# Two stages of a two-layer trunk in another order: the first key product beside the gates, and RWKV's weight halves cast one segment earlier

## Chip, core and metric

The kernel runs on one core of one Trainium2 chip, as one launch. The metric is the device time of that launch in microseconds (us); lower is better. Before the change it is 2180.25 us, the median of three runs (2178.22 to 2181.9).

The engines are named as the profile names them: PE is the matrix engine (PEld its weight loads), DVE the vector engine, ACT the scalar engine, POOL the fourth compute engine, and SP the engine whose queue issues nearly all DMAs here. Each engine works through its own instructions in program order; it waits, with everything queued behind, whenever the next instruction needs something that another engine or a DMA has not yet delivered.

## What is computed

One inference step of a two-layer trunk, for one prompt of 16 + 1024 tokens and for 8 decoding sequences of 8 tokens (1104 token columns in all, cut into three segments of 384, 384 and 336). Layer 0 is gated DeltaNet, layer 1 is RWKV-7. Cut to what matters here:

```python
def gdn_mixer(xn, S0, conv_buf, w_in, ...):          # layer 0
    proj = xn @ w_in
    qkv, z, b, a = ...                               # q, k, v, output gate, two gates per head
    qkv, new_buf = causal_conv(qkv, conv_buf, conv_w)   # 4 taps, then silu
    q, k = l2norm(q), l2norm(k)
    beta = jax.nn.sigmoid(b)
    g = -jnp.exp(a_log) * jax.nn.softplus(a + dt_bias)
    gc = jnp.cumsum(g)                               # within a chunk
    decay = jnp.exp(gc[i] - gc[j])
    A = I + strict(beta * k @ k.T * decay)
    u, wk = triangular_solve(A, ...)                 # per chunk and head
    ...                                              # state recurrence over the chunks
def rwkv_mixer(xn, ...):                             # layer 1
    xs = xn + (xprev - xn) * mu                      # six token-shift mixes
    r, k, v, z = (xs[m] @ w_rkvz[m] for m in range(4))
    ...                                              # decay, delta recurrence, group norm, gate, w_o
```

## The kernel before

All activations are kept with the tokens along the free axis. A product with a weight matrix is written as three passes that together give nearly full float32 precision: the weight is split into a rounded part `whi` and a rest `wlo`, the input likewise (`xa`, `xc` and others hold the parts), and one 128-wide block of output channels over one segment is 24 matmuls (8 blocks of the contraction, three passes each). A weight half (4 blocks, tile `wraw`, 256 KB) is loaded by SP, cast to `whi` by ACT (line 87) and subtracted to `wlo` by POOL (line 91).

**The start of layer 0** (`layer0`). The input rows are normed and transposed, then `gates` (lines 350 to 406) makes the per-head decays. Its first step multiplies all three segments by the 48 gate columns (tile `d`, copied to `rows`); its second transposes `rows` (PE tile `fgt`) and computes `g` on DVE and ACT (`gx`, `gy`, `gb`, `gs`); its third takes the cumulative sums on PE (`fgc`, `mge`) and copies them to `gc` on DVE (line 388); its fourth transposes `gc` (PE tile `fgr`), copies that to `gr` on DVE (lines 401 and 402) and writes it to DRAM (`drow`, SP lines 405 and 406). From `drow` SP loads, broadcast over rows, the tile `E` (line 649); POOL masks it (affine selects, lines 653 to 658), ACT takes the exponentials, and DVE multiplies it by the key scores `fsc` (line 712). The result goes through DRAM (`ltd`, line 718) into the tile `invA`, of which `inverse32` (lines 573 and 575) makes 32-wide triangular inverses in 31 steps of two DVE instructions each. DVE copies the result (line 743), SP sends it through DRAM (`g_t`, `T1n`, lines 746 and 749), and PE merges the blocks (tile `rY`), after which PE's products go on.

Beside that, the first head pair's products run: `keys` (PE tile `dk`), `gdn_queries` (`dq`), `gdn_values` (`dv`). Each segment's result is copied by ACT to `raw`, convolved (one tap on ACT, three on DVE, tile `cvy`, line 526), and squashed to `K`, `Q` or `vt` (line 532). The order is set by hand: PE and ACT run under a manual schedule, `self.slot` counts half segments of products, and `gdn_events` fastens the other steps (the gate steps, the scores, the inverse) to slot numbers. The first product starts at slot -24. `history` and `history_turn` load and turn the old convolution rows (`hist`, `histT`). The convolution tiles live in the pool `fp`, which is opened by `gdn_front` after the input rows (`x0` to `x8`) have been given up.

**The projections of layer 1** (`layer1`, `projections`). 24 blocks (m, k) of the weights for r, v and z run on PE, tile `d`, each for two or three segments. The weights come by halves: `weights(n + 1, 0)` is called at a block's first segment and `weights(n + 1, 1)` at its last, each a load by SP, a cast by ACT and a subtraction by POOL; `whi` and `wlo` have three buffers each, which all halves share. The results are copied to `ev` by ACT (line 2354) and stored. Into this stream a planner's numbers (`LOWER`, `END`) put the making of the RWKV inverses (tiles `sldcak`, `ssq`, `fL`). The recurrence itself, the wave, follows (`wave`), and opens with transfers that SP issues in program order: folds (`fld2c`, `fldrv`), `AR`, `BK`, `rTT`, and the old states `sn`.

## Time and profile before

| | |
|---|---|
| runs of the kernel | 2180.25 us median (2178.22 to 2181.9, three runs) |
| profiled execution | 2173.21 us, of which the span is 2171.5 us |
| mean granted PE clock | 0.982 |
| busy: PE, DVE, ACT, POOL | 2046.2, 1583.4, 1283.1, 834.9 us |
| instructions in the span | 54811 |
| DMA traffic | 292.52 MB, 135 GB/s on average |

The span is what the trace covers; the profiled execution is 1.7 us longer. A row of a timeline reads: start, busy time, engine and line, operation, output and inputs, tile shapes, count of like instructions merged, and in brackets the engine's idle time just before and what ended it. A row of windows reads: the stretch, its length, then busy time and instruction count of PE, PEld, DVE, ACT and POOL, the granted PE clock, the share of time that the DMA engines were busy, and GB/s.

### The profile page before, as it was taken

The page shows a single profiled execution, that of the slowest core. Times are in us where ns is not written, and L with a number is a line of the kernel's source. Part 1 is how long each engine was busy: PE and PEld are TensorE (multiplying, and loading weights), DVE is VectorE, ACT ScalarE, POOL GpSimd, SP SyncE. Part 2 cuts the span into 40 slices and gives each one's busy share as a digit, 9 for nine tenths or more (in the row PEclk, how much of TensorE's full clock was granted, in tenths as well). Part 3 has the DMA queues.
Part 4 walks back from the last instruction along what each step waited for, and adds up shares of the span by engine and source line. Part 5 has one row for each costly group of instructions (what it writes and reads, how often), then busy time and mean ns, then how long its engine had stood idle before and what let it go on. Part 6 is the DMA issues. An engine that isn't in the chain of part 4 may idle for free. (4 is left out here: it accounts for less than half of the span.)

```text
span 2171.5 us, 54811 instructions
## 1 busy us (share of the span) xinstructions
PE 2046.2 (94%) x20418; PEld 1905.8 (88%) x20418; DVE 1583.4 (73%) x4212; ACT 1283.1 (59%) x3750; POOL 834.9 (38%) x1136
## 2 busy tenths in 40 slices
PE   6969899999999999999999999889899999999997
PEld 5959899999999999998899999889798988888876
DVE  6968879698888979795334676757979557767755
ACT  4536565656565665656533365664747446677774
POOL 3523334334343333334231352344524254444444
PEclk9979999999999999999999999999999999999999
DMA  3424343424333333335345115655555486677754
GB/s 120 122 58 105 77 108 90 118 79 107 90 97 106 106 97 104 97 102 159 106 129 135 63 54 191 220 160 174 169 180 158 117 224 175 188 234 225 228 178 139
DMA packets 430724, 292.52 MB, mean 135 GB/s; under 512 B 147337, under 2 KB 413050, under 8 KB 430458
## 3 DMA queue, kind: packets, MB, share of 16 engines
q1 hardware_dynamic: 430458, 289.02, 46.2%
q8 instruction: 161, 2.64, 0.5%
q14 instruction: 105, 0.86, 0.1%
HBM read 197.55 MB, written 91.37 MB: 133 GB/s over the span
## 5 line engine op out<-in xcount | busy, mean ns | idle before, releaser
L91 POOL TENSOR_TENSOR wlo<-wraw,whi 128x512 fp32r<-128x512 f32 (+1 forms) x246 | 331.1, 1348 | 465.6 <-ACT whi L87 413.9
L77 PE MATMUL d<-xc,whi 128*128 128x384 f32 (+2 forms) x1006 | 279.5, 337 | 4.8 <-ACT whi L87 4.1
L526 DVE SCALAR_TENSOR_TENSOR cvy<-raw,cw,cvy 128x408 f32<-128x408 f32 (+2 forms) x288 | 199.0, 692 | 17.1 <-ACT cvy L63 15.7
L87 ACT CAST whi<-wraw 128x512 fp32r<-128x512 f32 (+1 forms) x246 | 149.8, 611 | 88.1 <-PE d L77 51.2
L77 PEld LDWEIGHTS d<-xc,whi 128*128 128x128 f32 (+1 forms) x1006 | 183.4, 189 | 7.8 <-ACT whi L87 4.8
L77 PE MATMUL d<-xc,wlo 128*128 128x384 f32 (+3 forms) x476 | 157.7, 340 | 2.7 <-POOL wlo L91 2.7
L77 PE MATMUL dz<-xc,whi 128*128 128x384 f32 (+1 forms) x480 | 153.9, 338 | 0.0
L77 PE MATMUL dv<-xc,whi 128*128 128x384 f32 (+1 forms) x480 | 152.4, 337 | 0.0
L77 PE MATMUL d<-xa,whi 128*128 128x384 f32 (+3 forms) x450 | 142.1, 340 | 4.5 <-ACT whi L87 1.7
L63 ACT ACTIVATE o<-rA,gcol 128x128 f32<-128x128 f32 x128 | 42.0, 366 | 116.9 <-DVE S L905 116.7
L573 DVE TENSOR_TENSOR invtmp<-invA,invT 72x31 f32<-72x31 f32 (+15 forms) x248 | 102.2, 412 | 3.2
L77 PE MATMUL dv<-xa,whi 128*128 128x384 f32 (+1 forms) x288 | 99.1, 344 | 0.0
L77 PE MATMUL dz<-xa,whi 128*128 128x384 f32 (+1 forms) x288 | 98.6, 342 | 0.0
L575 DVE TENSOR_TENSOR invT<-invT,invtmp 72x31 f32<-72x31 f32 (+15 forms) x248 | 95.0, 383 | 3.3
L77 PEld LDWEIGHTS d<-xc,wlo 128*128 128x128 f32 (+1 forms) x476 | 89.3, 189 | 6.8 <-POOL wlo L91 3.6
L77 PEld LDWEIGHTS dz<-xc,whi 128*128 128x128 f32 x480 | 89.4, 189 | 4.6 <-issue 4.5
L77 PEld LDWEIGHTS d<-xa,whi 128*128 128x128 f32 (+1 forms) x450 | 83.9, 189 | 8.2 <-issue 3.7
L77 PEld LDWEIGHTS dv<-xc,whi 128*128 128x128 f32 x480 | 89.2, 188 | 1.4 <-issue 1.4
L77 PE MATMUL d<-xa,wlo 128*128 128x384 f32 (+3 forms) x252 | 84.9, 337 | 1.4 <-POOL wlo L91 1.4
L77 PE MATMUL dk<-xc,whi 128*128 128x384 f32 (+1 forms) x240 | 79.3, 349 | 0.0
L77 PE MATMUL dq<-xc,whi 128*128 128x384 f32 (+1 forms) x240 | 77.0, 338 | 0.0
L1335 DVE SCALAR_TENSOR_TENSOR mixs<-xb,pcol,mixs 128x320 f32<-128x320 f32 (+2 forms) x96 | 68.6, 725 | 5.9 <-ACT mixs L63 5.6
(542 smaller groups left out, 6801.0 us busy)
## 6 DMA issues: line engine op xcount, KB each, us to landing
wraw<-in_gdn_w_in SPq DMA_DIRECT2D x96, 256.0 KB
wraw<-in_rwkv_w_rkvz SPq DMA_DIRECT2D x80, 256.0 KB
Sb<-in_state_gdn SPq DMA_DIRECT2D x64, 256.0 KB
sldcak<-cakd SPq DMA_DIRECT2D x24, 576.0 KB
wraw<-in_rwkv_w_o SPq DMA_DIRECT2D x42, 256.0 KB
E<-drow SPq DMA_DIRECT2D x24, 384.0 KB
attn<-drow SPq DMA_DIRECT2D x24, 384.0 KB
wraw<-in_gdn_w_out SPq DMA_DIRECT2D x36, 256.0 KB
```

The costliest lines, as they stand in the source:

```text
L63: return self.nc.scalar.activation(out, in_, func, bias=bias, scale=scale, **kw)
L77: self.nc.tensor.matmul(out, lhsT, rhs, start=start, stop=stop)
L87: nc.scalar.copy(hi, x)
L91: e.tensor_tensor(lo, x, hi.bitcast(F32), op=ALU.subtract)
L526: nc.vector.scalar_tensor_tensor(y[0][:, 0:wd], raw[:, k:k + wd], cw[k], y[0][:, 0:wd], op0=ALU.mult, op1=ALU.add)
L573: nc.vector.tensor_tensor(tmp, A[:, j, j + 1:32].unsqueeze(2).broadcast_to([nb, n, m]), Tv[:, j, 0:m].unsqueeze(1).broadcast_to([nb, n, m] ...
L575: nc.vector.tensor_tensor(Tv[:, j + 1:32, 0:m], Tv[:, j + 1:32, 0:m], tmp, op=ALU.subtract)
L1335: nc.vector.scalar_tensor_tensor(x[:, f:], xb[:, 8 + a + f:8 + b], mu, x[:, f:], op0=ALU.mult, op1=ALU.add)
```

## The change

Two independent parts. Line numbers after the change are 1 to 27 higher than before.

**Part A, start of layer 0.** `gates` now yields after each of its three segments. `layer0` runs the gates' first segment, then both halves of the first key product's first segment, then the gates' other two segments, then the three remaining gate steps, then the rest of the key product; `products` skips this product, so the slots start at -18 and all later slot numbers stay. For this the first key weights are loaded ahead of the input norm, and the convolution tiles get a pool of their own (`gconv`, opened first), so that they need not wait for the input rows' room; `x0` to `x8` are allocated ahead.

**Part B, projections of layer 1.** The load (`fetch`) is separated from the cast and the subtraction (`weights`), which run at high priority. Every second block's second half has its own pair of buffers, so there are four in all; `weights(n + 1, 1)` runs at segment 1 (of 0 to 2, or of 0 and 1 for z), and the next block's first half is already loaded then.

```diff
@@ gates
     for s, (c0, n) in enumerate(SEGS):
         p = self.dense(w, 64, xh, xl, s)
         nc.scalar.copy(rows[:, c0:c0 + n], p[0:48, 0:n])
-    yield
+        yield
@@ history, history_turn, last_tokens, conv (hist, histT, last, raw, cvy alike)
-        r = t(self.fp, [108, 128], "hist", 1)[0:96]
+        r = t(self.cvp, [108, 128], "hist", 1)[0:96]
@@ build
+            self.cvx = ExitStack()
+            self.cvp = self.cvx.enter_context(tc.tile_pool(name="gconv", bufs=1, side="right", reuse_waits="tile"))
@@ layer0
         self.gates_open(gates)
+        self.raw_weights(1024)
         self.input_norm(hi, lo)
         self.inp.close()
         self.gdn_front(front)
-        self.raw_weights(1024)
...
-        gate = self.gates(kh, kl)
-        next(gate)
...
         self.history_turn(G[0].H)
+        gate, first = self.gates(kh, kl), G[0].keys(0)
+        for n in range(3):
+            next(gate)
+            if not n:
+                next(first)
+                next(first)
+        for _ in range(3):
+            next(gate, None)
+        for _ in first:
+            pass
...
             for n, (_, f) in enumerate(todo):
-                yield from f(todo[n + 1][0] if n + 1 < len(todo) else None)
+                if n:
+                    yield from f(todo[n + 1][0] if n + 1 < len(todo) else None)
...
-        before(-24)
+        before(-18)
...
-            self.slot = -24
+            self.slot = -18
@@ layer1
-        def weights(n, h, elo="first"):
+        raw = {}
+
+        def fetch(n, h):
             if n < 25:
                 m, k = (todo + [(3, 0)])[n]
-                (hi,), (lo,) = self.load_w(..., 4, elo=elo)
-                W[n, h] = hi, lo
+                raw[n, h] = self.load_w(..., 4, later=True)[0]
+
+        def weights(n, h):
+            if n < 25:
+                if (n, h) not in raw:
+                    fetch(n, h)
+                own = n % 2 and h
+                hi, lo = W[n, h] = [t(self.own if own else self.wp, [128, 4, 128], a, 1 if own else 3, F32R) for a in ("whi", "wlo")]
+                with tc.high_priority():
+                    self.split(raw.pop((n, h)), hi, lo)
...
-        ip = pool("rinv", ctx)
+        ip = self.own = pool("rinv", ctx)
...
                     if s == 0:
                         weights(n + 1, 0)
-                    if s == segs[m] - 1:
+                        fetch(n + 1, 1)
+                    if s == 1:
                         weights(n + 1, 1)
+                        if n < 23:
+                            fetch(n + 2, 0)
```

How the instructions stand now, at three places. A row gives line, operation, output and inputs with buffer numbers, and size; `x2` and the like merge equal neighbours. In all, the order differs by few instructions: the work is the same but for one or two weight halves' position.

**Place 1, start of layer 0.** On PE, before, the cumulative sums stand in the middle of the key product's second segment (`dk_589`), between its two halves:

```order
L77 MATMUL dk_589<-xc_107,whi_375 128x384
L77 MATMUL fgc_606<-g_556,upto_27_152 128x16
L77 MATMUL fgc_606<-g_556,upto_28_153 128x128
L77 MATMUL fgc_606<-g_556,past_29_154 128x16
L77 MATMUL fgc_606<-g_556,past_30_155 128x128
L77 MATMUL mge_613<-gs_564,ones_82 128x144
L77 MATMUL mge_613<-g_556,ones_82 128x128
L77 MATMUL dk_589<-xc_107,whi_379 128x384
L77 MATMUL dk_589<-xc_107,wlo_380 128x384
```

Now they stand in the first query product (`dq_728`), behind the whole key product:

```order
L77 MATMUL dq_728<-xa_112,wlo_621 128x384
L77 MATMUL dq_728<-xc_116,whi_620 128x384
L77 MATMUL dq_728<-xc_116,whi_660 128x384
L77 MATMUL fgc_584<-g_573,upto_27_155 128x16
L77 MATMUL fgc_584<-g_573,upto_28_156 128x128
L77 MATMUL fgc_584<-g_573,past_29_157 128x16
L77 MATMUL fgc_584<-g_573,past_30_158 128x128
L77 MATMUL mge_591<-gs_581,ones_91 128x144
L77 MATMUL mge_591<-g_573,ones_91 128x128
L77 MATMUL dq_728<-xc_116,wlo_661 128x384
```

So 12 matmuls of `dk`'s second segment, the 24 of its third and 13 of `dq`'s first segment have come ahead of `fgc` (and 32 `dk` matmuls ahead of the last `fgt`). The two `fgr` rows, before between `dk`'s second and third segment, now stand in the middle of `dq`'s second segment. On DVE, before, `gc` and `gr` follow directly on the first key segment's convolution (`cvy_582`):

```order
L526 SCALAR_TENSOR_TENSOR cvy_582<-raw_521,cw_404,cvy_582 128x408 x3
L388 COPY gc_611<-fgc_606 128x9x8x2
L401 COPY gr_641<-fgr_638 128x128
L402 COPY gr_641<-fgr_638 16x128
L526 SCALAR_TENSOR_TENSOR cvy_633<-raw_587,cw_404,cvy_633 128x384
L532 SCALAR_TENSOR_TENSOR K_648<-raw_521,cvy_582 128x64
L532 SCALAR_TENSOR_TENSOR K_648<-raw_521,cvy_582 128x320
L526 SCALAR_TENSOR_TENSOR cvy_633<-raw_587,cw_404,cvy_633 128x384
L507 COPY raw_718<-histT_508 128x8x3
```

Now they stand behind the convolutions of all three key segments (`cvy_637` and `cvy_677` are the second and third) and the first tap of the query's (`cvy_756`):

```order
L533 SCALAR_TENSOR_TENSOR K_645<-raw_502,cvy_637 128x384
L527 SCALAR_TENSOR_TENSOR cvy_677<-raw_642,cw_407,cvy_677 128x336 x3
L389 COPY gc_589<-fgc_584 128x9x8x2
L533 SCALAR_TENSOR_TENSOR K_684<-raw_642,cvy_677 128x336
L527 SCALAR_TENSOR_TENSOR cvy_756<-raw_725,cw_407,cvy_756 128x408
L402 COPY gr_601<-fgr_598 128x128
L403 COPY gr_601<-fgr_598 16x128
L527 SCALAR_TENSOR_TENSOR cvy_756<-raw_725,cw_407,cvy_756 128x408
L703 SCALAR_TENSOR_TENSOR fsc_786,kq_692<-fsc_786,ident_83 128x128
```

DVE's set of instructions from there to the inverse's end (line 743) is the same as before; the scores of the second segment (line 702) now come ahead of the first multiplication of `E`.

**Place 2, start of layer 1's projections, ACT.** Before, the copy of the first result (`ev_18355`) stands ahead of a table load and the norms of the first inverse (`sldcak`, `ssq`):

```order
L87 CAST xh_2705_15356<-mixs_19021 128x384
L87 CAST xh_2707_15358<-mixs_19071 128x384
L2354 COPY ev_18355<-d_18296 128x384
L63 ACTIVATE mixs_19175<-xb_2604_14337,omu_411 128x64
L63 ACTIVATE mixs_19175<-xb_2604_14337,omu_411 128x320
L63 ACT_TABLE_LOAD
L63 ACTIVATE sldcak_18319<-sldcak_18319 128x383
L63 ACTIVATE ssq_18325<-sldcak_18319 128x384
L63 ACTIVATE mixs_19231<-xb_2602_14335,omu_411 128x384
```

Now a weight cast (`whi_18382`) comes first, and the copy (`ev_18361`) stands behind the table load:

```order
L87 CAST whi_18382<-wraw_18359 128x512
L87 CAST xa_112<-mixs_18278 128x336
L63 ACTIVATE mixs_19083<-xb_2603_14340,omu_414 128x64
L63 ACTIVATE mixs_19083<-xb_2603_14340,omu_414 128x320
L87 CAST xh_2705_15360<-mixs_19027 128x384
L87 CAST xh_2707_15362<-mixs_19083 128x384
L63 ACT_TABLE_LOAD
L63 ACTIVATE sldcak_18323<-sldcak_18323 128x383
L63 ACTIVATE ssq_18329<-sldcak_18323 128x384
L63 ACTIVATE mixs_19181<-xb_2604_14341,omu_414 128x64
L63 ACTIVATE mixs_19181<-xb_2604_14341,omu_414 128x320
L2381 COPY ev_18361<-d_18300 128x384
```

From here on each cast on ACT, each `wlo` on POOL and each load on SP of the projections stands at the same place as before but holds the next half.

**Place 3, opening of layer 1's wave, SP.** Before, one load of a weight half (`wraw_23107`) stands among the loads of the states `sn`, and two follow them (`ev_23101` is a result of the last projection):

```order
L1959 DMA sn_23182<-in_state_rwkv 64x4x64
L205 DMA wraw_23107<-in_rwkv_w_rkvz 128x4x128
L1959 DMA sn_23182<-in_state_rwkv 64x4x64
L2355 DMA zd<-ev_23101 128x384
L1959 DMA sn_23182<-in_state_rwkv 64x4x64 x2
L205 DMA wraw_23198<-in_rwkv_w_rkvz 128x4x128
L205 DMA wraw_23204<-in_rwkv_w_rkvz 128x4x128
L1555 DMA fldrv_23265<-rvd 128x2x384
L1709 DMA AR_23267<-abd 128x384
L1710 DMA BK_23268<-abd 128x6x64
```

Now the four `sn` come first, and two weight halves stand ahead of the first `rTT` and the folds:

```order
L1960 DMA sn_23186<-in_state_rwkv 64x4x64 x4
L2382 DMA zd<-ev_23105 128x384
L205 DMA wraw_23202<-in_rwkv_w_rkvz 128x4x128
L205 DMA wraw_23208<-in_rwkv_w_rkvz 128x4x128
L1730 DMA rTT_3859_23171<-ttd 128x384
L1556 DMA fld2c_23267<-cakd 128x2x384
L1556 DMA fldrv_23269<-rvd 128x2x384
L1710 DMA AR_23271<-abd 128x384
L1711 DMA BK_23272<-abd 128x6x64
```

On POOL, the `wlo` that stood ahead of the copies to `DC` (which need `fld2c`) is gone from there, so that the next `wlo` stands behind them.

More of the change, by code (lines that the diff above doesn't have):

```diff
@@ L270, in input_open @@
         self.xrows = []
+        self.xt = [self.t(self.lp, [128, D], f"x{q}") for q in range(9)]
     def input_load(self, qs):
         for q in qs:
-            x = self.t(self.lp, [128, D], f"x{q}")
+            x = self.xt[q]
             self.xrows.append((x, self.rows_of_x(x, q)))
@@ L481, in history_turn @@
         self.transpose(p[:, 0:96], H.raw)
-        H.old = self.t(self.fp, [128, 4, 8, 3], "histT", 1)
+        H.old = self.t(self.cvp, [128, 4, 8, 3], "histT", 1)
         self.nc.vector.tensor_copy(H.old.rearrange("p u b r -> p (u b r)"), p[:, 0:96])
@@ L488, in last_tokens @@
         self.transpose(p[0:108, 0:128], H.last.rearrange("p u b -> p (u b)"))
-        ls = self.t(self.fp, [108, 128], "hist", 1)
+        ls = self.t(self.cvp, [108, 128], "hist", 1)
         nc.vector.tensor_copy(ls, p[0:108, 0:128])
@@ L503, in begin @@
             if u == 0:
-                H.last = t(self.fp, [128, 4, 27], "last", 1)
-            raws[0] = raw = t(self.fp, [128, 411], "raw", 3)
+                H.last = t(self.cvp, [128, 4, 27], "last", 1)
+            raws[0] = raw = t(self.cvp, [128, 411], "raw", 3)
             sv = raw[:, 0:88].rearrange("p (b r) -> p b r", r=11)
@@ L512, in follow @@
             if s < 2:
-                raws[s + 1] = t(self.fp, [128, 411], "raw", 3)
+                raws[s + 1] = t(self.cvp, [128, 411], "raw", 3)
                 nc.gpsimd.tensor_copy(raws[s + 1][:, 0:3], prev)
@@ L522, in taps @@
                 nc.gpsimd.tensor_copy(H.last[:, u, 0:24].rearrange("p (b r) -> p b r", r=3), sv[:, :, 8:11])
-            y.append(t(self.fp, [128, 408], "cvy", 2))
+            y.append(t(self.cvp, [128, 408], "cvy", 2))
             self.act(y[0][:, 0:wd], raw[:, 0:wd], AF.Identity, scale=cw[0])
@@ L2205, in layer0 @@
         front.close()
+        self.cvx.close()
         before(999)
@@ L2253, in layer1 @@
         self.rwkv_masks(self.ev, None)
+        t = self.t
         todo = [(m, k) for m in (0, 2, 3) for k in range(8)]
@@ L2263, in part @@
             self.mix_part(m, k, c0, c0 + n, xb[k], *self.slots[order[m][k]], self.ev, lows[m])
-        def weights(n, h, elo="first"):
+        raw = {}
+        def fetch(n, h):
             if n < 25:
                 m, k = (todo + [(3, 0)])[n]
-                (hi,), (lo,) = self.load_w(self.i["rwkv_w_rkvz"][0, m][512 * h:512 * h + 512, 128 * k:128 * k + 128], 4, elo=elo)
-                W[n, h] = hi, lo
+                raw[n, h] = self.load_w(self.i["rwkv_w_rkvz"][0, m][512 * h:512 * h + 512, 128 * k:128 * k + 128], 4, later=True)[0]
+        def weights(n, h):
[6 more added lines that the diff above has]
+                    self.split(raw.pop((n, h)), hi, lo)
         def between(k):
@@ L2365, in layer1 @@
         b_now = [-1]
-        t = self.t
         with tc.manual_schedule(engines={mybir.EngineType.PE}):
```

## The prediction

> **What bounds the kernel now.** The page's first table says PE: 2046.2 of 2171.5 us. That is an average; what counts is where PE is not busy, and whether the change touches that. I read the windows first (length, then busy time and count of PE, PEld, DVE, ACT, POOL, then PE clock, DMA share, GB/s).
>
> ```profile
> 0.00:41.00 41.00, 22.20 (x130) 18.57 (x131) 28.80 (x60) 22.82 (x43) 14.99 (x47) 0.96 0.52 157
> 41.00:60.00 19.00, 18.56 (x122) 17.47 (x121) 7.71 (x20) 9.07 (x20) 2.50 (x6) 1.00 0.10 28
> 60.00:128.19 68.19, 50.60 (x357) 47.60 (x355) 66.09 (x177) 29.22 (x81) 32.22 (x46) 0.92 0.36 96
> 60.00:70.00 10.00, 9.93 (x62) 9.61 (x61) 9.75 (x19) 5.55 (x16) 6.98 (x14) 1.00 0.96 290
> 113.00:133.00 20.00, 0.38 (x4) 0.14 (x2) 15.16 (x39) 1.10 (x6) 3.43 (x3) 0.61 0.19 49
> 1745.00:1780.00 35.00, 31.62 (x303) 27.24 (x303) 21.19 (x48) 15.76 (x37) 17.18 (x23) 0.95 0.99 271
> ```
>
> Part A lies in the rows up to 133, the opening of RWKV's wave, which part B's loads touch, in the last. From 113 to 133 PE stands still, and the timelines of PE and DVE say for what:
>
> ```profile
> 133.43 0.31 PE L77 MATMUL rY<-T1n,E 32*32 32x32 f32 x2 [20.05 <-DMA T1n<-g_t]
> 70.77 1.65 DVE L712 SCALAR_TENSOR_TENSOR E<-fsc,bp,E 128x128 f32<-128x128 f32 x6
> 89.70 0.17 DVE L573 TENSOR_TENSOR invtmp<-invA,invT 72x31 f32<-72x31 f32 x1
> 128.19 1.03 DVE L743 COPY invA<-invT 72x1024 f32<-72x1024 f32 x1
> ```
>
> PE waits 20.05 us for the inverse, which ends on DVE at 128.19, and 5.2 us of copy and DMA later PE goes on. So until 133 **DVE is the bound**, not PE. DVE is busy 66.09 of 68.19 us after 60, and its timeline shows no wait there; between 41 and 60 it is busy 7.71 of 19, idle 11.3. Moving key matmuls ahead gains only if it moves the inverse's end; PE's own time in this stage is covered by the 20 us.
>
> **Part A, step by step.** The key product's 36 matmuls and 13 of the query product come ahead of the cumulative sums `fgc`.
>
> ```profile
> 47.23 0.38 PE L74 MATMUL fgt<-ident,rows 48*128 48x48 f32 x3 [0.44 <-ACT rows L362]
> 51.88 0.60 PE L77 MATMUL fgc<-g,upto 128*128 128x16 f32 x4
> 55.45 0.40 PE L77 MATMUL dk<-xa,whi 128*128 128x336 f32 x1
> 59.21 0.33 PE L77 MATMUL dq<-xa,whi 128*128 128x384 f32 x1
> 60.96 0.33 PE L77 MATMUL dq<-xa,wlo 128*128 128x384 f32 x1
> 39.47 0.37 PE L77 MATMUL d<-xa,whi 128*64 128x336 f32 x1 [0.72 <-ACT xa L305]
> 33.12 0.39 PE L77 MATMUL d<-xc,whi 128*64 128x384 f32 x1 [0.61 <-DVE xc L309]
> ```
>
> The third segment's 24 matmuls take 59.21 - 55.45 = 3.8 us. The row at 60.96 is the eleventh of `dq`, ten intervals after 59.21: 0.175 each. So `fgc` moves by 25 x 0.175 + 3.8 = 8.2 us, less the PE idle that the earlier `dk` matmuls fill, at most 0.61 + 0.72 + 0.44 = 1.8: `fgc` at about 58.3 instead of 51.88. The cumulative sum is then copied on DVE, in before at once, now behind three taps of the third key segment, which wait for ACT:
>
> ```profile
> 54.62 0.30 DVE L388 COPY gc<-fgc 128x144 f32<-128x144 f32 x1
> 63.62 3.58 DVE L526 SCALAR_TENSOR_TENSOR cvy<-raw,cw,cvy 128x336 f32<-128x336 f32 x3
> 55.24 1.28 ACT L63 ACT_TABLE_LOAD   x1
> 56.54 0.66 ACT L63 ACTIVATE eglb<-mge 128x272 f32<-128x272 f32 x1
> 57.97 0.62 ACT L63 ACTIVATE cvy<-raw,cw 128x384 f32<-128x384 f32 x1
> 58.49 0.53 ACT L63 ACTIVATE raw<-cvy 128x408 f32<-128x408 f32 x1
> 56.06 0.36 SPq L405 DMA_DIRECT2D drow<-gr  x1
> 62.14 1.14 POOL L653 TENSOR_SCALAR_AFFINE_SELECT E<-E 128x768 f32<-128x768 f32 x1 [0.48 <-DMA E<-drow]
> 64.53 0.85 POOL L653 TENSOR_SCALAR_AFFINE_SELECT E<-E 128x768 f32<-128x768 f32 x1
> 68.16 1.86 ACT L63 ACTIVATE E<-E,gcol 128x128 f32<-128x128 f32 x6
> 69.33 0.30 DVE L702 SCALAR_TENSOR_TENSOR fsc<-fsc,ident 128x128 f32<-128x128 f32 x1
> ```
>
> In the new order ACT has, after the third tap of the second segment (about 58.2, just ahead of `gs`), a table load 1.28, a tanh 0.53 and a first tap 0.6: 60.6. Three taps at 0.6 (as for the other forms; 3.58 for three is a disturbed row, below) end at 62.4: `gc` there, 8 us later than in before. `fgr` is in PE's order 20 `dq` matmuls behind `mge`, at about 63.3, so it isn't late. Then `gr` stands on DVE behind `K` and the query's first tap, which needs ACT's next steps (a tanh 0.53, `eglb` and three short ones about 1.0, the query's copies about 0.5, a tap 0.6): 65.0; the tap 0.6 and the copies 0.5 on DVE follow, and `drow` is sent at about **66.0 instead of 56.06**.
>
> From there the trace has one path: `drow` out, `E` in, POOL's select at 62.14 (6.1 us after `drow`), 1.14 for it, an exponential of 0.31 (1.86 for six): the first multiplication of `E` can start 7.6 us after `drow`. In before that was 63.7, and DVE came to it at 70.77, 7 us of slack. Now it is 73.6 at the soonest. At 60 to 70 the DMAs are loaded, so I take 0.7 more, **74.3, or +3.5 us**; the ends are +0.3 (`gc` not held by the taps, `drow` at 63.5) and +5.5.
>
> Behind that DVE has the same work left as in before's 57.4 us (70.77 to 128.19), less what is already done, plus new waits. Done already: the second segment's scores, three at 0.3, each with a read of 0.1, and three small steps, -1.6. New waits: two sets of `E` now follow each other, and a set needs 0.85 on POOL and six exponentials on ACT against 1.65 on DVE, +1.0; the first step of the inverse (89.70) comes to wait for `invA`, issued at 86.04 in before, +1.1; two taps that DVE reaches early, +0.8. The waits are estimates from the order of these rows; together 0 to 4. The front's sum: 3.5 - 1.6 + 2.9 = **+4.8 us**, with ends -1 and +8. PE's stall gets shorter by what PE arrives later, and PE goes on 4.8 us later. Nothing behind takes that back, since the recurrence needs the inverse.
>
> One row could be worse than taken. The three taps at 63.62 took 3.58 us instead of 1.8, beside POOL's selects on `E` (from 62.14); the new selects fall beside the multiplications of `E`, and if these were held alike the front would cost 1.8 more. The row at 70.77 speaks against: six in 1.65 us, beside other work of POOL. [...]
>
> **Part B, projections.** The rows of waits that it can remove, and the one that it adds:
>
> ```profile
> 1419.03 0.44 PE L77 MATMUL d<-xa,whi 128*128 128x384 f32 x1 [0.27 <-ACT ev L2354]
> 1425.53 0.69 PE L77 MATMUL d<-xc,whi 128*128 128x384 f32 x1 [4.13 <-ACT whi L87]
> 1427.56 0.69 PE L77 MATMUL d<-xc,wlo 128*128 128x384 f32 x1 [1.35 <-POOL wlo L91]
> 1418.51 0.47 ACT L2354 COPY ev<-d 128x384 f32<-128x384 f32 x1
> 1419.70 1.28 ACT L63 ACT_TABLE_LOAD   x1
> 1553.31 0.44 PE L77 MATMUL d<-xa,whi 128*128 128x384 f32 x1 [1.68 <-ACT whi L87]
> 1554.85 0.69 PE L77 MATMUL d<-xa,wlo 128*128 128x384 f32 x1 [1.10 <-POOL wlo L91]
> 1574.56 0.77 PE L77 MATMUL fL<-sldcak 64*32 64x64 f32 x45 [0.95 <-DVE sldcak L1617]
> ```
>
> At the start the second half is cast a step earlier: 4.13 + 1.35 = 5.5 us gone. But the copy `ev`, for which PE waits already 0.27 (its PSUM buffer), now stands behind a cast 0.5, the table load 1.28, two norms 0.8 and a mix 0.8: +3.4. Net **-2.1**. At 1553 the two waits (2.8) go as well, but PE then comes 2.8 us sooner to `fL`, which waits for DVE's `sldcak` already: I take 0. Elsewhere every cast keeps its place and holds the next half, so nothing moves. Ends: -8.3 if all four waits go and nothing comes, +1 if the new wait is longer.
>
> **The wave's opening.** SP takes its rows in order:
>
> ```profile
> 1748.33 0.54 SPq L1729 DMA_DIRECT2D rTT<-ttd  x1
> 1750.83 1.61 POOL L91 TENSOR_TENSOR wlo<-wraw,whi 128x512 fp32r<-128x512 f32 x1 [0.96 <-ACT whi L87]
> 1753.39 0.42 PE L77 MATMUL zz<-xa,whi 128*128 128x336 f32 x1 [1.08 <-DVE zst L1294]
> 1762.48 0.77 PE L74 MATMUL fVT<-ident,fldrv 128*128 128x128 f32 x3 [1.11 <-DVE G L1758]
> ```
>
> `rTT` and the folds now stand behind two weight halves, the second of which needs a buffer that POOL's `wlo` of 1750.83 to 1752.44 frees. Issued at 1748.33 before, at 1752.4 then: 4.1 us, with 271 GB/s in flight. PE waits there already for what comes of such loads (1.08 and 1.11). So 0 to +4.1; I take **+2.3**, a little over half, since PE has some work at hand.
>
> **Sum.** +4.8 - 2.1 + 2.3 = +5.0. The profiled execution (2173.21, span 2171.5) is 7 us below the median, with the same program; the difference is added to the median: **2185.2 us**.
>
> **Rivals.**
> - *The same time* (2181.5): the front gives only +2.5 (`drow` near 64.5, or the new waits fall together), and the opening +1: 2.5 - 2.1 + 1 = +1.4. It decides by when `gc` is copied. For it: DVE's order leaves 3 us of play around 62. Chance 0.35.
> - *Faster* (2175): the earlier convolution of the first key segment fills the 11.3 us that DVE is idle from 41 to 60, so DVE does more before the inverse. That decides if `drow` is sent before about 62.5, so that `E` is ready by the 70 us at which DVE wants it; then the front gives -2, part B -3. The row of windows 41 to 60 speaks for it, the place of `gr` behind eight DVE rows against. Chance 0.10.
> - *Much slower* (2190): the multiplications of `E` or the inverse's loads are held by busy DMAs (share 0.96 from 60 to 70), front +7, opening the whole +4: +9 or +10. Chance 0.10.
> - *Part B doesn't do what it says*: the order of casts is unchanged but for the ends, so the waits might stay: then 2187. It lies within the forecast's own range.
>
> The forecast has 0.45, with 0.2% (4.4 us, about what a measurement of this kernel can tell from no change) inside its range: faster 0.10, same 0.35, slower 0.55. The range takes in the faster rival's near side and the much slower one: 2176 to 2191.
>
> **What would show it.** `drow` on SP near 66, and DVE's first `E` multiplication near 74.3 with a wait on ACT or POOL ahead of it; the copy on line 743 (there 744) near 133 and PE's restart near 138. If `drow` goes out before 63, part A's argument is wrong at `gc`. In the projections: no wait for `whi` near 1430, but one of about 3.5 us for `ev`. At the opening: `rTT` behind the weight loads, and longer waits at `zz`, `fVT` or the states.

## The result, and the profile after

| | before | after |
|---|---|---|
| median, 19 runs each | 2180.25 us (2172.53 to 2184.76) | 2185.34 us (2176.34 to 2190.41) |
| ratio, with its 95% interval | | 1.0028 (1.0018 to 1.0037) |
| profiled execution (span) | 2173.21 us (2171.5) | 2190.41 us (2188.7) |
| mean granted PE clock | 0.982 | 0.978 |

The changed kernel is slower, by 0.28% or 6 us by the ratio and by 5.1 us by the two medians. The two traces are 17 us apart, because the one of before lies near the bottom of its kernel's runs and the one of after is the slowest of its own. So a stage is compared by its rows and its waits, not by the two ends.

The windows of after, with the columns of before's:

```profile
41.00:60.00 19.00, 19.00 (x123) 17.97 (x123) 9.73 (x22) 8.05 (x15) 2.57 (x7) 1.00 0.07 18
60.00:70.00 10.00, 7.45 (x49) 6.89 (x47) 5.96 (x26) 2.56 (x8) 0.58 (x3) 1.00 0.31 103
113.00:133.00 20.00, 5.01 (x30) 4.45 (x28) 18.52 (x50) 3.52 (x12) 3.53 (x3) 0.73 0.12 33
```

From 41 to 60 PE is now never idle. From 60 to 70, where before all four engines were at work, POOL now works 0.58 us (6.98 before), ACT 2.56 (5.55) and DVE 5.96 (9.75), and the DMAs' share falls from 0.96 to 0.31: the decays have not arrived. The timelines of after, engine by engine, show the path that the prediction followed:

```profile
56.19 0.61 PE L77 MATMUL fgc<-g,upto 128*128 128x16 f32 x4
58.49 1.77 DVE L527 SCALAR_TENSOR_TENSOR cvy<-raw,cw,cvy 128x336 f32<-128x336 f32 x3
60.17 0.30 DVE L389 COPY gc<-fgc 128x144 f32<-128x144 f32 x1
63.60 0.28 DVE L402 COPY gr<-fgr 128x128 f32<-128x128 f32 x1
63.91 0.36 SPq L406 DMA_DIRECT2D drow<-gr  x1
69.81 0.87 POOL L654 TENSOR_SCALAR_AFFINE_SELECT E<-E 128x768 f32<-128x768 f32 x1 [7.23 <-DMA E<-drow]
71.65 0.64 DVE L713 SCALAR_TENSOR_TENSOR E<-fsc,bp,E 128x128 f32<-128x128 f32 x2 [3.33 <-ACT E L63]
72.75 1.81 DVE L713 SCALAR_TENSOR_TENSOR E<-fsc,bp,E 128x128 f32<-128x128 f32 x6 [0.46 <-ACT E L63]
89.62 0.19 DVE L574 TENSOR_TENSOR invtmp<-invA,invT 72x31 f32<-72x31 f32 x1 [2.22 <-DMA invA<-ltd]
131.43 1.03 DVE L744 COPY invA<-invT 72x1024 f32<-72x1024 f32 x1
136.71 0.31 PE L77 MATMUL rY<-T1n,E 32*32 32x32 f32 x2 [17.83 <-DMA T1n<-g_t]
```

`drow` goes out at 63.91 instead of 56.06, DVE has a new wait of 3.33 us for the exponentials of `E`, the inverse ends at 131.43 instead of 128.19, and PE goes on 3.28 us later. To see what DVE did with the time, I cut it at its first multiplication of `E` and at the first step of the inverse. The windows of before, then of after (the third number group behind the length is DVE):

```profile
0.00:70.77 70.77, 51.46 (x315) 46.42 (x316) 46.89 (x99) 38.20 (x80) 25.23 (x67) 0.98 0.46 140
70.77:89.70 18.93, 17.22 (x129) 15.95 (x128) 18.84 (x60) 10.78 (x30) 12.11 (x19) 1.00 0.35 77
89.70:128.19 38.49, 22.68 (x165) 21.27 (x163) 36.87 (x98) 12.12 (x34) 12.36 (x13) 0.86 0.21 57
```

```profile
0.00:71.65 71.65, 51.06 (x317) 45.61 (x317) 45.24 (x107) 35.13 (x70) 21.71 (x64) 1.00 0.39 118
71.65:89.62 17.97, 13.89 (x73) 13.55 (x74) 13.09 (x44) 12.05 (x37) 10.86 (x19) 0.83 0.54 142
89.62:131.43 41.81, 27.38 (x217) 25.17 (x215) 40.40 (x104) 14.18 (x38) 14.26 (x16) 0.89 0.22 60
```

Ahead of the first multiplication DVE did 8 instructions more in 1.65 us less. Between the cuts it did 16 fewer and stood still 4.88 us instead of 0.09. What it could not do there stands beside the inverse, which took 41.81 us instead of 38.49. Over the three rows DVE is busy 3.87 us less and idle 7.12 us more; the difference, 3.2, is how much later the inverse ends, and PE goes on as much later.

In layer 1 the two waits for weights near 1430 are gone, and the copy `ev` behind the table load has come in their place. Timelines of after, ACT and PE:

```profile
1425.48 1.28 ACT L63 ACT_TABLE_LOAD   x1
1428.31 0.46 ACT L2381 COPY ev<-d 128x384 f32<-128x384 f32 x1
1428.82 0.69 PE L77 MATMUL d<-xa,whi 128*128 128x384 f32 x1 [3.77 <-ACT ev L2381]
1577.10 1.35 PE L77 MATMUL fL<-sldcak 64*32 64x64 f32 x45 [3.60 <-DVE sldcak L1618]
```

The longest two rows of PE's waits from 1404 to 1740 (engine, what it waited for, us in total, times, longest), of before and of after:

```profile
PE d L77 <- ACT whi L87: 5.8, 2, 4.1
PE d L77 <- POOL wlo L91: 3.7, 4, 1.3
```

```profile
PE fL L77 <- DVE sldcak L1618: 5.2, 2, 3.6
PE d L77 <- ACT ev L2381: 4.4, 2, 3.8
```

All rows of this view add up to 17.8 us before and 19.7 after: 9.5 us of waits for weights went, and others took their place. At the wave's opening SP's timeline of after and PE's waits from 1740 to 1800 read:

```profile
1758.63 1.37 SPq L205 DMA_DIRECT2D wraw<-in_rwkv_w_rkvz  x2
1760.05 0.50 SPq L1730 DMA_DIRECT2D rTT<-ttd  x1
```

```profile
PE dsn L74 <- DMA sn<-in_state_rwkv: 2.7, 1, 2.7
PE zz L77 <- DVE zst L1295: 1.5, 1, 1.5
```

Two weight halves stand ahead of `rTT`, and the waits of this stretch add up to 5.4 us (3.4 before).

### The profile page after: what moved, and what is told of

Same layout as the page of the kernel before. It is cut to its first block, busy times and chain, and to the rows that moved or that the text cites. A ratio compares the mean times of both kernels' runs of the same rounds, so it can differ in the third digit from the quotient of the medians.

```text
span 2188.7 us, 54828 instructions
## 1 busy us (share of the span) xinstructions
PE 2055.5 (94%) x20418; PEld 1912.7 (87%) x20418; DVE 1571.5 (72%) x4212; ACT 1284.0 (59%) x3750; POOL 834.9 (38%) x1136
## 5 line engine op out<-in xcount | busy, mean ns | idle before, releaser
L527 DVE SCALAR_TENSOR_TENSOR cvy<-raw,cw,cvy 128x408 f32<-128x408 f32 (+2 forms) x288 | 188.6, 655 | 22.8 <-ACT cvy L63 21.3
L63 ACT ACTIVATE mixs<-xb,omu 128x64 f32<-128x64 f32 (+3 forms) x128 | 61.8, 521 | 18.3 <-DVE xc L91 8.4
```

The costliest lines, as they stand in the source:

```text
L63: return self.nc.scalar.activation(out, in_, func, bias=bias, scale=scale, **kw)
L527: nc.vector.scalar_tensor_tensor(y[0][:, 0:wd], raw[:, k:k + wd], cw[k], y[0][:, 0:wd], op0=ALU.mult, op1=ALU.add)
```

## The experiments

Behind the first comparison (19 runs of each kernel) all times are medians of ten or twelve runs, each beside 35 runs of the kernel before on the same chip. PE's restart is the start of the row `rY`; the last two columns are the sums of PE's waits in the two stretches above, each from one trace.

| kernel | us | before beside it | ratio (95%) | PE's restart | waits 1404 to 1740 | 1740 to 1800 |
|---|---|---|---|---|---|---|
| before | | | | 133.43 | 17.8 | 3.4 |
| the change | 2185.34 | 2180.25 | 1.0028 (1.0018 to 1.0037) | 136.71 | 19.7 | 5.4 |
| the change again | 2181.60 | 2179.55 | 1.0010 (0.9995 to 1.0024) | 136.31 | 17.7 | 5.0 |
| part A alone | 2181.58 | 2179.55 | 1.0013 (0.9998 to 1.0028) | 135.65 | 18.7 | 6.7 |
| part B alone | 2175.99 | 2179.55 | 0.9987 (0.9972 to 1.0002) | 133.20 | 19.1 | 4.2 |
| part B alone, again | 2174.80 | 2175.10 | 0.9990 (0.9975 to 1.0004) | 133.13 | 15.4 | 5.4 |
| A, gate steps in their slots | 2175.26 | 2179.55 | 0.9981 (0.9968 to 0.9994) | 133.61 | 20.3 | 3.6 |
| the same again | 2176.15 | 2175.10 | 1.0000 (0.9983 to 1.0016) | 136.20 | 20.1 | 4.3 |
| A, gate steps a slot later | 2176.58 | 2174.81 | 1.0003 (0.9988 to 1.0017) | 138.22 | 16.1 | 2.9 |
| gate steps in slots, with B | 2173.47 | 2174.81 | 0.9995 (0.9982 to 1.0009) | 135.80 | 14.3 | 3.6 |
| the change, `ev` by DVE | 2178.16 | 2174.81 | 1.0017 (1.0001 to 1.0032) | 137.55 | 19.3 | 4.7 |
| B, `LOWER` later | 2174.75 | 2174.81 | 1.0002 (0.9987 to 1.0016) | 133.08 | 17.3 | 4.4 |
| before, two hops more | 2173.53 | 2175.10 | 0.9996 (0.9979 to 1.0013) | 136.05 | 17.1 | 3.4 |
| before, four hops more | 2176.84 | 2175.10 | 1.0008 (0.9991 to 1.0025) | 137.45 | 16.0 | 2.5 |

### The two parts apart, and the change again

For part A alone, the changed kernel with before's projections in layer 1:

```diff
-                raw[n, h] = self.load_w(..., 4, later=True)[0]
...
+                (hi,), (lo,) = self.load_w(..., 4, elo=elo)
+                W[n, h] = hi, lo
...
-                    if s == 1:
+                    if s == segs[m] - 1:
```

> Part A alone (layer 0's start in the new order, layer 1 as before). Theory 1 (the decays' way through DRAM is sent too late): DVE's first multiplication of E waits for ACT by about 3 us as in the changed kernel, drow is sent near 64, PE restarts at rY near 136.7 instead of 133.4, and the time is 3 to 5 us over before (ratio 1.0014 to 1.0023). Theory 2 (the loss sits in layer 1): the front is within 1 us of before's, and so is the time.

Measured: 1.0013, just under the 1.0014 to 1.0023 of the first theory, with an interval that takes in no change. Timelines of DVE and PE in part A alone:

```profile
70.76 0.64 DVE L713 SCALAR_TENSOR_TENSOR E<-fsc,bp,E 128x128 f32<-128x128 f32 x2 [2.94 <-ACT E L63]
1424.20 0.69 PE L77 MATMUL d<-xa,whi 128*128 128x384 f32 x1 [3.75 <-ACT ev L2367]
```

The first row is the front's new wait, as in the change. The second was not expected there: PE waits 3.75 us for `ev`, though this kernel has before's projections. So the copy's place behind the table load comes with part A, which alters nothing in layer 1's code; what moved is the order of ACT's instructions there (the table load at 1421.05, the copy at 1423.69). Of part A it is the place of the gate steps that decides: in the kernels of the next section with these steps back in their slots the copy stands ahead of the table load again (at 1420.04 and 1422.19).

For part B alone, before with the change's projections:

```diff
+                raw[n, h] = self.load_w(..., 4, later=True)[0]
...
-                    if s == segs[m] - 1:
+                        fetch(n + 1, 1)
+                    if s == 1:
                         weights(n + 1, 1)
```

> Part B alone (layer 1's weight halves earlier, layer 0 as before). Theory 1: PE restarts at rY near 133.4 as before; the waits for whi and wlo near 1425 (5.5 us) are gone; in this program's order the copy ev stands ahead of the table load, so no wait of 3.8 us for it; what is gained is taken by the waits of fL for sldcak near 1575, and the opening of the wave loses about 2: the time is 2 below to 2 above before. Theory 2: part B alone carries the loss, 4 to 6 us over before.

Measured: 0.9987, or 2.8 us below before, where the forecast ended at 2. PE's timeline of part B alone, and two windows of it:

```profile
1422.35 0.44 PE L77 MATMUL d<-xa,whi 128*128 128x384 f32 x1 [0.92 <-ACT ev L2368]
1549.65 0.77 PE L77 MATMUL fL<-sldcak 64*32 64x64 f32 x45 [1.59 <-ACT sldcak L63]
1570.22 1.35 PE L77 MATMUL fL<-sldcak 64*32 64x64 f32 x45 [3.61 <-DVE sldcak L1617]
```

```profile
1415.00:1435.00 20.00, 18.64 (x157) 17.18 (x155) 16.14 (x26) 17.69 (x42) 12.66 (x17) 1.00 0.47 151
1565.00:1590.00 25.00, 21.39 (x314) 19.41 (x313) 19.42 (x47) 9.12 (x23) 7.04 (x9) 0.86 0.46 144
```

The same windows of before:

```profile
1415.00:1435.00 20.00, 14.25 (x115) 13.02 (x116) 14.78 (x27) 16.89 (x39) 10.75 (x13) 0.83 0.41 143
1565.00:1590.00 25.00, 24.05 (x395) 21.85 (x395) 21.63 (x52) 12.25 (x30) 10.45 (x12) 1.00 0.50 157
```

Without part A the copy waits 0.92 us only, and part B does what it says: from 1415 to 1435 PE is busy 4.39 us more, and its clock stays at 1.00 where before's falls to 0.83. From 1565 to 1590 it gives this back: the wait for `sldcak` is 3.61 us instead of 0.95, PE is busy 2.66 us less, and now the clock falls here, to 0.86.

The change itself was run once more, unaltered.

> The changed kernel a second time, to see which of its trace's differences recur. Theory 1: rY near 136.7, the wait for ev near 1428 and the longer waits of fL near 1577 and of the states near 1770 all recur, since they follow from the order; the 8 us that the first trace lost behind 1900 don't. Rival: they recur too, and belong to the change. Time 1.002 to 1.004 of before.

Measured: 1.0010, below the 1.002 to 1.004 that was forecast. The front's rows recur (a wait of 2.71 us for `E`, PE's restart at 136.31), and so does the wait for `ev`, 3.77. Most of what the first trace lost behind the projections does not: from PE's first `zz` behind 1740 to the end of the span it is 423.0 us in before, 433.6 in the first trace of the change and 426.3 in the second.

Part B alone was run a second time as well.

> The kernel of e2 again: 0.9987 (0.9972 to 1.0002) there. Theory 1 (part B by itself gains a little, what it wins near 1425 being mostly lost at fL): 0.998 to 1.000. Rival (it costs): over 1.000. The waits of fL near 1550 and 1570 (1.6 and 3.6 us) recur, and none for whi near 1425.

Measured: 0.9990, after 0.9987. Neither interval leaves 1 out. At the opening SP's order is the change's in both, yet PE's wait for the states (`dsn`) is 0.4 us in the first and 3.0 in the second; part A alone, with before's order, has 2.3.

### The gates' place

Part A, with the rest of the key product and the gate steps fastened to slots again; only the gates' and the key product's first segments stay swapped:

```diff
-        for _ in range(3):
-            next(gate, None)
-        for _ in first:
-            pass
...
-                if n:
-                    yield from f(todo[n + 1][0] if n + 1 < len(todo) else None)
+                yield from f(todo[n + 1][0] if n + 1 < len(todo) else None) if n else first
...
-        before(-18)
+        before(-22)
...
-            self.slot = -18
+            self.slot = -22
```

> Part A, with the early first segment of the key product kept, but the remaining gate steps and the rest of the key product back in the hand-made slots (fgc between the halves of dk's second segment). Theory 1: gc is copied ahead of the second and third key segment's taps, drow is sent between 56 and 60, the first multiplication of E has no wait on ACT of over 0.5 us, PE restarts between 132.5 and 134.5, and the time is within 2 us of before. Rival (the early segment itself, with its own pool and its earlier weight load, costs the time): drow is early, but PE restarts near 136 all the same, and the time is 3 to 5 us over before.

Measured: 0.9981. SP's and PE's timelines of it:

```profile
57.32 0.36 SPq L406 DMA_DIRECT2D drow<-gr  x1
51.44 0.88 PE L77 MATMUL fgc<-g,upto 128*128 128x16 f32 x4 [3.60 <-DVE g L377]
```

`drow` leaves 6.6 us sooner than in the change, DVE's wait for `E` is gone, and PE restarts at 133.61, as in before. The price is a wait of 3.60 us at `fgc`, since `g` is not ready there. I took it for a kernel that beats before, and ran it once more.

> The kernel of e3 again, for its time: 0.9981 (0.9968 to 0.9994) there. If that is real, 0.9975 to 0.9990 here; if it was chance, 0.999 to 1.001. PE restarts at 133 to 136, with a wait of 3.6 us for g at fgc.

Measured: 1.0000, PE's restart at 136.20, the same wait of 3.60 us at `fgc`. The gain was not confirmed. The later restart does not come from the gate steps: the whole front began later in this trace (DVE's `gx`, the first step on `fgt`, at 50.13 instead of 47.88), and from `gx` to the restart it is 86.07 us here and 85.73 in the first trace (85.77 in before).

To be rid of that wait, the last two gate steps, one slot later:

```diff
-        for u in (-23.4, -21.4, -20.4):
+        for u in (-23.4, -20.4, -19.4):
```

> Part A with the gate steps in the slots, fgc and fgr one slot (12 matmuls) later than in e3: drow goes out near 60 instead of 57.3 (e3) or 63.4 (e1). Theory 1 (there is slack of about 6 us between E's arrival and DVE's need; only what exceeds it costs): no wait on ACT of over 0.5 us before the first multiplication of E, PE restarts between 133.3 and 135, time within 2 us of e3's, ratio 0.997 to 1.0. Rival (each us by which drow is late costs a us): PE restarts near 136, ratio 1.000 to 1.002.

Measured: 1.0003, and PE's restart at 138.22, outside of the 133.3 to 135 that were forecast. The wait did not go: it is 4.20 us at `fgc` (54.97). It holds the key product, and the taps that follow it, and the front began 2 us later here too (`gx` at 49.91), so this run tells nothing clean about the decays alone. The hops below do.

The change, with the gate steps in their slots by the first edit of this section:

> The changed kernel with the gate steps and the rest of the key product back in the slots (the edit of e3) and part B kept. Theory 1 (only the place of the gate steps costs, and both parts are good without it): PE restarts near 133.5, the copy ev stands ahead of the table load, and the time is 4 to 8 us below before (ratio 0.9965 to 0.998). Theory 2 (the two gains don't add, since fL and the wave's opening take part B's back): ratio 0.998 to 1.0.

Measured: 0.9995, outside of the 0.9965 to 0.998 that a sum of the two gains asked for, and PE restarts at 135.80 instead of 133.5. The copy `ev` stands ahead of the table load, as both theories had it, and PE waits 0.91 us for it. One of the two gains was not confirmed when it ran again (1.0000), so this run does not tell whether gains add.

### Two suspected waits in layer 1

If the wait for `ev` is a real part of the loss, it goes when DVE makes the first copy:

```diff
-                        nc.scalar.copy(f_[:, 0:w], p[:, 0:w])
+                        (nc.scalar.copy if n or s else nc.vector.tensor_copy)(f_[:, 0:w], p[:, 0:w])
```

> The changed kernel with one instruction on another engine: the first result of layer 1's projections is copied to ev by DVE, so that it doesn't stand behind ACT's table load. Theory 1 (the wait of 3.8 us near 1428 is that copy's place, and what goes there is lost again further on): the wait falls below 1.2 us, but the waits of fL near 1560 to 1577 stay at 5 us in all or grow, and the time is that of the changed kernel within 2 us (ratio 1.000 to 1.003). Theory 2 (that wait is a real part of the loss): the time falls by 3 to 4 us, ratio 0.999 to 1.001.

Measured: 1.0017. The waits for `ev` are 0.86 and 1.53 us instead of 3.77, and the clock from 1415 to 1435 stays at 1.00 (0.83 in the change). But PE waits 3.60 us for `sldcak` at 1572.92, its waits in the stretch are 19.3 us, and the kernel is as slow as the change. The gain of one wait is taken by the next.

If part B loses its gain to `sldcak` coming late, the use of it can be moved one or two steps on, at three places:

```diff
-        LOWER = (13, 19, 25, 31, 35, 41, 47, 53, 59, 63, 69, 76, 82, 88, 92, 98, 104, 110, 116, 120, 126, 132, 137, 142)
+        LOWER = (13, 19, 25, 31, 35, 41, 47, 53, 59, 63, 71, 78, 83, 88, 92, 98, 104, 110, 116, 120, 126, 132, 137, 142)
```

> Part B alone, and three numbers of the planner raised by 1 or 2 units (the steps of the tenth to twelfth lower part, 69, 76, 82 to 71, 78, 83), so that PE meets fL later. Theory 1 (what part B gains near 1425 is lost near 1550 to 1577 because PE now comes to fL before sldcak is ready): the wait of 3.6 us near 1570 falls below 1, the shift stays at -5 us behind 1577, and the time is 2 to 4 us below part B alone (ratio 0.997 to 0.998). Theory 2: the wait moves to the next step of the inverse (mYU or fL again), same time as part B alone (0.998 to 1.0).

Measured: 1.0002. PE's timeline:

```profile
1551.70 0.77 PE L77 MATMUL fL<-sldcak 64*32 64x64 f32 x45 [2.42 <-issue]
1570.23 0.77 PE L77 MATMUL fL<-sldcak 64*32 64x64 f32 x45 [3.27 <-DVE sldcak L1617]
```

The first theory failed: the wait near 1570 is 3.27 us, hardly less than the 3.61 of part B alone, and near 1551 one of 2.42 us stands where part B alone had 1.59. So in either order PE comes to these products before `sldcak` is ready.

### The decays' lateness alone

The last pair leaves every product of before in its place, and sends `drow` through DRAM two or four times more, so that only the decays are late:

```diff
+        for q in range(2):
+            c = self.dram([8, 9, 2, 128], f"drow{q}")
+            nc.sync.dma_start(c.rearrange("j t h k -> (j t h) k"), self.drow.rearrange("j t h k -> (j t h) k"))
+            self.drow = c
```

> The kernel before, with two copies from DRAM to DRAM put between drow and its use, so that only the decays' way gets longer; the products keep their order. Theory 1 (the decays have some 6 us of slack, and only what exceeds it costs): E is loaded 4 to 6 us later (near 63 instead of 58.6), DVE's first multiplication of E waits less than 0.7 us, PE restarts within 0.7 us of 133.4, time within 2 us of before. Rival (any lateness of the decays costs): restart 3 us or more later.

> The same with four copies. Theory 1: E is loaded near 67 or 68, beyond the slack; DVE waits 2 to 5 us for it, PE restarts 2 to 5 us later than 133.4, as in the changed kernel (136.7), and the time is 2 to 4 us over before, though no matmul has moved. Rival (the changed kernel's loss comes from the moved products, not from the decays): restart within 1 us of 133.4.

Measured: 0.9996 and 1.0008. The timelines of SP, DVE and PE with two hops:

```profile
63.41 1.29 SPq L653 DMA_DIRECT2D E<-drow  x3
71.26 0.64 DVE L716 SCALAR_TENSOR_TENSOR E<-fsc,bp,E 128x128 f32<-128x128 f32 x2 [2.14 <-ACT E L63]
136.05 0.28 PE L77 MATMUL rY<-T1n,E 32*32 32x32 f32 x2 [20.27 <-DMA T1n<-g_t]
```

With four:

```profile
67.98 1.30 SPq L653 DMA_DIRECT2D E<-drow  x3
73.37 0.35 DVE L716 SCALAR_TENSOR_TENSOR E<-fsc,bp,E 128x128 f32<-128x128 f32 x1 [3.41 <-ACT E L63]
137.45 0.28 PE L77 MATMUL rY<-T1n,E 32*32 32x32 f32 x2 [17.85 <-DMA T1n<-g_t]
```

In before `E` was loaded at 58.55. The fronts of both kernels begin as before's does (`gx` at 47.42 and 47.78, 47.66 in before). Loads 4.9 and 9.4 us later move PE's restart by 2.6 and 4.0 us; the change, with its load at 65.49 (6.9 later), moves it by 3.3, between the two. So the lateness of the decays is enough to explain the front's loss, and no more matmuls need to be moved for it. The forecast that two hops would cost under 0.7 us at PE's restart failed: the slack that it took for before is not there. The windows from the start to the inverse's end, of before and with four hops, show the other side:

```profile
0.00:128.19 128.19, 91.36 (x605) 83.64 (x605) 102.61 (x255) 61.10 (x143) 49.70 (x98) 0.94 0.37 106
0.00:132.15 132.15, 92.64 (x605) 85.02 (x605) 97.97 (x256) 61.33 (x143) 46.42 (x98) 0.94 0.36 104
```

The same DVE work, and one record more, takes 4.64 us less once the decays are late. The ratios of both runs lie within what a measurement can tell from no change, so the front is read from its rows.

## Why the prediction came out, step by step

**The bound of the front: right.** PE moved ahead and gained nothing by it; DVE's end of the inverse set its restart in every kernel. In the four traces of kernels with part A's gates as they stand in the change, PE restarts at 135.65 to 137.55 (mean 136.56); in before and three traces of part B, at 133.08 to 133.43 (mean 133.21). So the front costs +3.3 us in the mean, instead of +4.8.

**`fgc`, `gc`, `drow`: right in order, 2 us too late in size.** Forecast 58.3, 62.4 and 66.0, measured 56.19, 60.17 and 63.91. `fgc` already carries the error. The windows from PE's first product of the gates (`d`) to `fgc`, of before and then of after, place it:

```profile
23.39:51.88 28.49, 26.31 (x166) 22.29 (x164) 19.27 (x48) 11.96 (x27) 7.47 (x11) 0.97 0.11 29
22.51:56.19 33.68, 33.33 (x215) 29.26 (x214) 25.29 (x57) 15.60 (x33) 11.91 (x19) 1.00 0.14 39
```

PE's idle time fell from 2.18 to 0.35 us, the 1.8 that the forecast allowed. But the 49 matmuls more took 7.0 us instead of 8.2 (the clock is 0.97 in the first row and 1.00 in the second), and the stretch began 0.9 us sooner, which differs from trace to trace: it begins at 22.46 to 23.86 over the four traces named above, and at 22.91 to 23.39 over those of before's front.

**`E`: the failed term.** It was forecast at 74.3, or +3.5, and measured at 71.65, or +0.9. From `drow` to the first multiplication it took 7.74 us, against 7.6 worked out and 0.7 added for busy DMAs, which weren't busy (share 0.31); the other 2.1 us came with `drow`. The slack of 7 us that the forecast gave before was wrong too: it ended the path at POOL's select and one exponential, but ACT was late there. Before's ACT timeline has the first pair:

```profile
67.07 0.68 ACT L63 ACTIVATE E<-E,gcol 128x128 f32<-128x128 f32 x2
```

At 67.4 the first factor was ready, so that 3.4 us of slack were left, not 7. And that slack shrinks as soon as `E` is late, since DVE then comes sooner: with two hops it came to `E` at 69.1 (71.26 less the wait of 2.14). The rival *faster* let `drow` be as late as 62.5; two hops correspond to 60.9 (63.41 less the 2.5 from `drow` to the load in before), and lose 2.6 us already. So that rival drew its condition too wide: 62.5 would have been too late.

**Work done ahead and new waits: forecast -1.6 and +2.9, measured -2.2 and +4.6.** Behind the first multiplication DVE was busy 53.49 us (13.09 + 40.40) instead of 55.71, and idle 6.29 us instead of 1.71. (The -2.2 also holds work that got shorter, as the next paragraph says.) The wait for `invA` was there, 2.22 us against 1.1 forecast. The two errors, at `E` and here, partly cancel: 0.9 + 2.4 = 3.3 where the sum had 3.5 + 1.3 = 4.8.

**A term that the sum lacked: DVE's own work got shorter.** The row that the forecast called disturbed, three taps in 3.58 us, takes 1.77 in the change. Over the whole front DVE's busy time falls by 3.87 us for the same instructions, and by 4.64 with four hops, where PE's order is before's. In before POOL's selects and copies ran beside these taps (POOL busy 3.58 of the 3.58 us from 63.62); when `E` is late, POOL stands idle there (0.00 of the 1.77 us from 58.49). That POOL causes it was not shown: it is the reading of these rows, in which the DMAs' share differs as well (1.14 and 0.00), and no run moved POOL's work alone. The first multiplications of `E` took 0.64 us for two, with POOL busy all that time, and 1.81 us for six, with POOL busy 1.57 of it, against 1.65 for six in before: not held, as the forecast had it.

**Projections: the rows right, the cause of one wrong.** The waits for `whi` and `wlo` near 1430 and 1553 went, and the wait for `ev` came, 3.77 us against 3.4 forecast. But the prediction laid it to part B, as the cast's new place in front of the copy. Part A alone has it (3.75), part B alone has not (0.92): it belongs to part A, and there to the place of the gate steps. With them in their slots it is 0.91 beside part B, and without part B PE waits for `whi` instead (4.46); with them a slot later it is back (3.54). That `fL` would take the gain at 1553 was right, and it took more: in part B alone also a good part of the gain near 1430. Over all traces PE's waits from 1404 to 1740 are 18.0 us in the mean with before's layer 1 (seven traces, 16.0 to 20.3) and 17.5 with part B's (seven, 14.3 to 19.7): -0.5, where the forecast had -2.1.

**Opening: +2.3 forecast, +0.9 measured.** The waits from 1740 to 1800 are 3.8 us in the mean of the seven traces with SP's order of before and 4.7 with the new one; in the two traces first compared, 3.4 and 5.4. SP's order changed as forecast. That it makes the longer wait for the states is not shown: 0.4 to 3.0 us stand under the same order.

**The sum.** +3.3 - 0.5 + 0.9 = +3.7 us by rows, +5.0 forecast; by time +5 to +6 in the first comparison and +2 in the second, whose interval takes in no change. The rows count waits alone, so they leave out what a lower clock behind a wait adds (last section). The forecast of 2185.2 is nearer to 2185.34 than its terms were to theirs: the front and the opening were too dear, the projections too cheap. So the mechanism was right in the main, and that the sum came so near is in part luck. The rival *same* (+1.4) named the right weak point, the moment when `gc` is copied, and its condition, `drow` near 64.5, was even met; the front cost more than its +2.5 because the waits behind `E` were longer than the forecast's.

**What stays open.** The parts' ratios alone, 1.0013 and 0.9987 or 0.9990, multiply to 1.0000 or 1.0003; both together gave 1.0028 and 1.0010. With these intervals the parts may add plainly or may not. The one candidate, the wait for `ev` that part A brings and that eats part B's gain, was tested: without it no fall of the time could be measured (1.0017, against 1.0028 and 1.0010). No kernel here is clearly faster than before: the one whose interval lay below 1 did not hold it when it ran again. The gate steps in slots with part B (0.9995), and part B alone, have ratios below both comparisons of the change, but their intervals overlap with that of the second.

## What to carry to other kernels

Slack is read from the last engine on the path, with all that is queued ahead of it there, not from the first transfer that lands; and when the engine on the path has less to do, or does it sooner, while the input is late, the slack shrinks. When a wait on the bounding engine is removed, look for the next wait on the same chain: here it took the gain 140 us later. A change at the start of a scheduled program can alter the order of a far later stage, so that a new wait should be laid to a part of the change only after each part has run alone.

## What was not expected of the hardware

**Two waits of PE cost more than their length.** The windows of after behind the waits at 1428.82 and 1577.10, each stretch at half clock followed by the one behind it:

```profile
1429.00:1433.00 4.00, 4.00 (x13) 4.00 (x14) 3.08 (x6) 4.00 (x10) 2.44 (x4) 0.51 0.37 139
1433.00:1437.00 4.00, 4.00 (x25) 4.00 (x24) 2.80 (x3) 3.34 (x8) 3.94 (x3) 1.00 0.51 169
1577.00:1583.00 6.00, 5.90 (x68) 5.33 (x69) 5.16 (x17) 1.35 (x4) 1.44 (x3) 0.50 0.66 210
1583.00:1587.00 4.00, 4.00 (x54) 3.79 (x54) 2.87 (x8) 1.53 (x3) 0.20 (x1) 0.98 0.25 99
```

After waits of 3.77 and 3.60 us PE runs at half clock for 4 and 6 us, 13 matmuls behind the first where the next 4 us hold 25. So, by an estimate from these rows, these waits cost some 2 and 3 us more than they show, while behind the wait of 0.92 us in part B alone the clock stays at 1.00. A shorter wait had it too: behind the wait of 2.67 us for `sn` in the trace of after (PE goes on at 1777.04) the clock is 0.50 from 1778 to 1780, while behind the wait of 2.12 us for `ev` in before (PE goes on at 1539.04) it stays at 1.00 (1537 to 1543). Length alone does not decide: in the wait of 3.77 us, from 1425.05 and 0.42 us behind one of 0.75, it is 0.57 from 1426 to 1427 and 0.50 behind; in that of 3.60, from 1573.50, it is 1.00 until 1576, 0.66 from 1576 to 1577 and 0.50 behind. By an estimate from these windows it was halved 1.1 us into the first and 2.8 us into the second, and 2.12 us in before did not halve it. It is back at 1.00 from 1433 to 1434 and at 0.93 from 1583 to 1584, 4 and 6 us after PE went on. The prediction priced waits by their length alone. In the projections this hits both sides: before pays it behind its wait of 4.13 us (0.83 from 1415 to 1435), part B alone behind `sldcak` (0.86 from 1565 to 1590).

**The same program's runs differ by 0.6 to 0.8%.** The 35 runs of before on one chip span 2171.34 to 2185.52 us, those on the two others 2167.96 to 2181.93 and 2165.23 to 2183.55. A change of a few us needs its stage's rows beside the medians.
